# A decoder layer in split fp32r on one core: Strassen's form for four of eight row pairs, another order of the SwiGLU chunks, deeper weight staging

## The chip, the core and the metric

The kernel runs on one core of a Trainium2 chip. The metric is device time in microseconds (us) of one execution. Three runs of the kernel before took 1230.06, 1230.45 and 1231.88 us; the median is 1230.45 us.

The engines are named as the profile names them: PE (TensorE matmul; PEld is its weight load, the load of the stationary operand), DVE (VectorE), ACT (ScalarE), POOL (GpSimd), SP (the queue that issues most loads).

## The reference

One layer on x of shape (1, 256, 2048) in fp32: a norm, one projection, three mixers side by side, an output projection, and a SwiGLU block. The change lies in the SwiGLU block, the last stage:

```python
h = rms_norm(x, ffn_norm_w[l])
gate, up = jnp.split(h @ w_ffn_in[l], 2, axis=-1)     # w_ffn_in: 2048 x 11264
x = x + (jax.nn.silu(gate) * up) @ w_ffn_out[l]       # w_ffn_out: 5632 x 2048
```

## The kernel before

**Three products for one.** Every fp32 operand is cut into a rounded part `hi` (fp32r) and the rest `lo`. A product is three matmuls, hi by hi, hi by lo and lo by hi (`triple`, L1364). ACT makes `hi` of a weight tile by a cast, DVE makes `lo` by a subtraction (`split`, L1326). A weight tile `raw` has 128 rows of two times 512 columns and comes from HBM in two loads of 256 KB on SP.

**The SwiGLU block.** The 5632 hidden columns are eleven chunks of 512. For a chunk, the gate and the up columns are formed for 256 tokens, that is two halves of 128. The inner dimension of 2048 is 16 row blocks of 128, taken as eight row pairs q = 0 to 7. The first chunk is done plainly (`first_pair`, L1406: 192 matmuls). The other ten go through `pair` (L1424): tokens by columns is a 2 x 2 block product (gate and up, first and second half of the tokens), with the two blocks of a row pair as the inner two. For the row pairs in `SEVEN` it takes Strassen's form (Winograd's variant): 7 products, 21 matmuls (kind "S"). For the others it takes 8 products, 24 matmuls (kind "N", four accumulators, one of them fed with differences of the token halves, `dif_h`). The S form needs sums of weight blocks, which DVE makes (`ta`, `tb` in `stage`), and sums of token blocks (`sums_h`, `sums_l`), which `ext_job` (L1372) makes once, while the first chunk runs.

An S unit fills four of the `hi`/`lo` tiles, an N unit two, a unit of the output product (kind "P", 12 matmuls) one. There are eight tiles of each in a ring, and six `raw` tiles.

After the products of a chunk, DVE adds the seven accumulators up (`c11`, `u2`, `u3`, `c22`), ACT takes the silu of the gate, and DVE multiplies by up, at the end of `pair`. `hid_cols` (L1396) is a generator that a `tick()` after each unit advances: it turns the product by transposes on PE (two sets of four, into a `gd` bank) and splits it into `hidh` and `hidl`, the stationary operands of the output product.

**The order of the work.** The engines run their instructions in the order of the source from L1266 on (`V.on = S.on = TE.on = True`). `PARTS = (12, 8, 8, 8, 8)` groups the 44 hidden blocks: three chunks, then the four output chunks n = 0 to 3 over those blocks, and then four times two chunks and four output chunks. So a group's output product comes straight behind its last chunk:

```python
for pi, (nh, ins_, outs_) in enumerate(work):
    for c, ul in enumerate(ins_):
        ... sgs = pair(ul); spawn(hid_cols(sgs, c))
    for n in range(4):
        ... stage(u + 1); triple(...)
```

`stage(u + 1)` puts the cast and the subtraction of unit u + 1 just ahead of the matmuls of unit u in every queue, so that weights are one unit ahead.

Of the kernel before, what the change touches and what calls it, by code (L numbers as in the profile page):

```python
# [8 lines left out]
F32 = mybir.dt.float32  # L9
F32R = mybir.dt.float32r  # L10
# [5 lines left out]
P = 128  # L16
# [137 lines left out]
def trunk(tc, A, out, dbg=None):  # L154
# [48 lines left out]
    cst = pc.tile([P, CONST.shape[1]], F32, name="cst")  # L203
    vec = pc.tile([P, NV], F32, name="vec")

    def C(name):
        o, n = CCOLS[name]
        return cst[:, o:o + n]
# [165 lines left out]
    xs1 = p_l.tile([P, T], F32, name="xs1")  # L374

# [94 lines left out]
    gns = prq.tile([P, 2, 32], F32, name="gns")  # L470
# [824 lines left out]
    work = []  # L1295
    h0 = 0
    for pi, nh in enumerate(PARTS):
        ins_ = [None if h0 + c == 0 else plan_in((h0 + c) // 4) for c in range(0, nh, 4)]
        work.append((nh, ins_, [plan_out(n, h0, nh) for n in range(4)]))
        h0 += nh  # L1300

    turn = {"raw": 0, "hi": 0, "lo": 0}
    homes = {"raw": (p_raw, F32, AHEAD), "hi": (p_hi, F32R, 4), "lo": (p_lo, F32R, 4)}

    def buf(kind):
        first, dt, more = homes[kind]
        turn[kind] += 1
        if turn[kind] % 2:
            return first.tile([P, 1024], dt, tag=kind, name=nm(kind))
        return pf.tile([P, 1024], dt, tag=kind, name=nm(kind), bufs=more)  # L1310

    loaded, ready_w = {}, {}
    at = {"load": 0, "stage": 0}

    def load_upto(i):
        while at["load"] <= min(i, len(queue) - 1):
# [7 lines left out]
            at["load"] += 1  # L1324

# [8 lines left out]
    def stage(i):  # L1334
        load_upto(i + 2)
        while at["stage"] <= min(i, len(queue) - 1):
            u = at["stage"]
            kind, r = queue[u][0], loaded.pop(u)
            if kind != "S":
                parts_ = [split(t) for t in r]  # L1340
                for x in parts_:
                    x[2]()
                ready_w[u] = [half(x, j) for x in parts_ for j in range(2)]
            else:
                b11, b12 = r[0][:, 0:512], r[0][:, 512:1024]
                b22 = r[1][:, 512:1024]
                s1, s0 = split(r[1]), split(r[0], 512)
                ta = pf.tile([P, 1024], F32, tag="ta", name=nm("ta"), bufs=1)
                tb = pf.tile([P, 2, 512], F32, tag="tb", name=nm("tb"), bufs=1)
                V.tensor_tensor(ta[:, 0:512], b22, b12, op=ALU.subtract)  # L1350
                V.tensor_tensor(ta[:, 512:1024], ta[:, 0:512], b11, op=ALU.add)
                s0[2]()
                s1[2]()
                sa = split(ta)
                V.tensor_tensor(tb, r[1].rearrange("p (a c) -> p a c", c=512),
                                ta[:, 512:1024].unsqueeze(1).to_broadcast([P, 2, 512]), op=ALU.subtract)
                sb = split(tb.rearrange("p a c -> p (a c)"))
                sa[2]()
                sb[2]()
                ready_w[u] = {"b11": half(s0, 0), "b21": half(s1, 0), "b22": half(s1, 1), "t3": half(sa, 0),  # L1360
                              "t2": half(sa, 1), "t4": half(sb, 0), "t1": half(sb, 1)}
            at["stage"] += 1
# [9 lines left out]
    def ext_job():  # L1372

        for q in range(KT // 2):
            x = pf.tile([P, 1024], F32, tag="ta", name=nm("xa"), bufs=1)[:, 0:2 * T].rearrange("p (k t) -> p k t", t=T)
            s_ = pf.tile([P, 2, 512], F32, tag="tb", name=nm("xs"), bufs=1)[:, 0, :].rearrange("p (k t) -> p k t", t=P)
# [10 lines left out]
            else:  # L1387
# [3 lines left out]
                h_, l_ = dif_h[:, i], dif_l[:, i]  # L1391
            S.copy(h_, s_)
# [3 lines left out]
    def hid_cols(sgs, c):  # L1396
        for i in range(2):
            yield
            b = gdbank(1)
            turned(sgs, i, b)  # L1400
            h_ = hh_[:, 4 * c + 2 * i:4 * c + 2 * i + 2, :].rearrange("p a t -> p (a t)")
            l_ = hl_[:, 4 * c + 2 * i:4 * c + 2 * i + 2, :].rearrange("p a t -> p (a t)")
            S.copy(h_, b)
            V.tensor_tensor(l_, b, h_.bitcast(F32), op=ALU.subtract)

    def first_pair(ul):  # L1406
        ug, uu = ul
        bg = proj(ug, hx)
        sgs = []
        for t in range(2):  # L1410
            sg = pf.tile([P, 512], F32, tag=f"sg{t}", name=nm("sg"), bufs=1)
            act(sg, bg[t], AF.Silu, scale=rs2[:, t:t + 1])
            sgs.append(sg)
        banks = [mmbank(), mmbank()]
        for i in range(len(uu)):
            if i == len(uu) - 1:
                stage(0)
            products(banks, uu, i, hx)
            tick()
        for t in range(2):  # L1420
            V.tensor_tensor(sgs[t], sgs[t], banks[t], op=ALU.mult)
        return sgs

    def pair(ul):  # L1424
# [3 lines left out]
        p2, p5, p4, p3 = mmbank(), mmbank(), mmbank(), mmbank()  # L1428
# [3 lines left out]
        n_units = [q for _, q in ul if q not in SEVEN]  # L1432
        for i, (u, q) in enumerate(ul):
            stage(u + 1)
            w = ready_w.pop(u)
# [39 lines left out]
    for pi, (nh, ins_, outs_) in enumerate(work):  # L1475
        hh_ = pf.tile([P, PARTS[0], T], F32R, tag="hidh", name=nm("hidh"), bufs=1)
        hl_ = pf.tile([P, PARTS[0], T], F32R, tag="hidl", name=nm("hidl"), bufs=1)
        for c, ul in enumerate(ins_):
            if ul is None:
                ej = spawn(ext_job())  # L1480
                sgs = first_pair(plan["first"])
                finish(ej)
            else:
                sgs = pair(ul)
            spawn(hid_cols(sgs, c))
        for n in range(4):
# [67 lines left out]
```

## Time and profile before

| | us |
|---|---|
| median of three runs | 1230.45 |
| profiled execution | 1230.36 |
| its span, first to last instruction | 1228.6 |
| PE busy | 1208.6 (98%) |
| DVE busy | 900.3 (73%) |
| ACT busy | 631.4 (51%) |
| first matmul of the SwiGLU block | at 492.57 |
| last matmul | at 1223.89 |

A busy PE means that a matmul was in it; a matmul of 512 columns is recorded with 0.39 us, but the next one starts 0.23 us after it. So what a matmul costs is read from the distance of starts, and a wait from a distance that is longer. All work of this kernel is recorded at line 108 (the queue's wrapper), so rows are told apart by the names of their tiles: `hTh` and `hTl` are the normed input, `hidh` and `hidl` the hidden values, `sg` and `u` the sums at a chunk's end.

### The profile page before, as it was taken

Reading aid. Unit: us, or ns where it says so; the run is one execution under the profiler, and the core shown is the slowest. Engines: PE = TensorE matmul, PEld = TensorE weight load, DVE = VectorE, ACT = ScalarE, POOL = GpSimd, SP = SyncE. Lnnn points to the kernel's source line nnn. Section 1 sums busy time; section 2 is a strip of 40 time slices with the busy share of each in tenths; the row PEclk is TensorE's granted clock in tenths of the full one; section 3 lists DMA queues with packets and bytes.
Section 4 is the critical chain, followed back from the end, with each engine's and each line's share of the span. In section 5 each row is a group of like instructions: output and inputs, shape, how many; then the busy total and the mean of one; then the engine's idle time right before and its main releaser. Section 6 shows DMA issues by size and latency. Waiting matters only on the chain.

```text
span 1228.6 us, 16426 instructions
## 1 busy us (share of the span) xinstructions
PE 1208.6 (98%) x5972; PEld 987.6 (80%) x5972; DVE 900.3 (73%) x1249; ACT 631.4 (51%) x877; POOL 5.8 (0%) x11
## 2 busy tenths in 40 slices
PE   9999999999999999989999999999999999999998
PEld 7877888788888878778878888788877888788877
DVE  8585965699465766768975689659875888678964
ACT  7664454665446556445554355436444445445632
POOL 0100000000000000000000000000000000000000
PEclk9999999999999999999999999999999999999999
DMA  9655564256555536556556575466555656466653
GB/s 321 210 146 157 169 198 116 74 152 187 172 165 187 169 128 197 157 180 217 177 167 222 186 229 176 158 218 202 183 187 173 216 180 222 145 209 212 192 171 117
DMA packets 129058, 222.49 MB, mean 181 GB/s; under 512 B 19632, under 2 KB 23856, under 8 KB 128976
## 3 DMA queue, kind: packets, MB, share of 16 engines
q1 hardware_dynamic: 120816, 217.17, 56.6%
q10 hardware_dynamic: 8160, 4.27, 1.2%
q8 instruction: 47, 0.77, 0.3%
q14 instruction: 35, 0.29, 0.1%
HBM read 218.50 MB, written 2.88 MB: 180 GB/s over the span
## 4 chain that ended last, share of the span: by engine, by line
PE 93%; DVE 3%; ACT 2%; DMA 1%; issue 1%; SPq 0%; DVEq 0%; ACTq 0%
PE mm L108 79%; PE rw L108 8%; PE gd L108 5%; DVE lo L108 2%; ACT hi L108 1%; DMA raw<-in_w_in 0%; DVE xs L108 0%; ACT hidh L108 0%; DVE xa L108 0%; DVE sg L108 0%; DVE u L108 0%; DMA vec<-in_vecs 0%; DVE hTl L108 0%; DVE xr L108 0%; ACT s L108 0%
## 5 line engine op out<-in xcount | busy, mean ns | idle before, releaser
L108 ACT CAST hi<-raw 128x1024 fp32r<-128x1024 f32 (+2 forms) x410 | 398.4, 1004 | 266.3 <-PE mm L108 118.8
L108 DVE TENSOR_TENSOR lo<-raw,hi 128x1024 fp32r<-128x1024 f32 (+2 forms) x410 | 464.4, 1164 | 90.8 <-ACT hi L108 90.1
L108 PE MATMUL mm<-hi,hTh 128*128 128x512 f32 (+1 forms) x872 | 338.9, 395 | 2.6 <-ACT hi L108 2.5
L108 PE MATMUL mm<-lo,hTh 128*128 128x512 f32 (+1 forms) x872 | 332.9, 388 | 4.3 <-DVE lo L108 4.3
L108 PE MATMUL mm<-hi,hTl 128*128 128x512 f32 (+1 forms) x872 | 332.4, 387 | 0.0
L108 PEld LDWEIGHTS mm<-lo,hTh 128*128 128x128 f32 x872 | 162.8, 188 | 38.3 <-DVE lo L108 6.4
L108 PEld LDWEIGHTS mm<-hi,hTh 128*128 128x128 f32 x872 | 162.6, 188 | 38.4 <-ACT hi L108 4.4
L108 PEld LDWEIGHTS mm<-hi,hTl 128*128 128x128 f32 x872 | 162.6, 188 | 33.9 <-issue 0.6
L108 PE MATMUL mm<-hi,hidh 128*128 128x512 f32 x352 | 138.1, 392 | 5.4 <-ACT hidh L108 5.4
L108 PE MATMUL mm<-lo,hidh 128*128 128x512 f32 x352 | 137.7, 391 | 1.8 <-DVE lo L108 1.8
L108 PE MATMUL mm<-hi,hidl 128*128 128x512 f32 x352 | 138.0, 392 | 0.0
L108 DVE SCALAR_TENSOR_TENSOR xr<-mm,rst,xr 128x512 f32<-128x512 f32 x40 | 30.0, 750 | 73.5 <-PE mm L108 73.5
L108 PEld LDWEIGHTS mm<-hi,hidh 128*128 128x128 f32 x352 | 66.1, 188 | 20.4 <-ACT hidh L108 7.3
L108 PEld LDWEIGHTS mm<-lo,hidh 128*128 128x128 f32 x352 | 66.1, 188 | 17.5 <-DVE lo L108 4.3
L108 PEld LDWEIGHTS mm<-hi,hidl 128*128 128x128 f32 x352 | 66.1, 188 | 16.8 <-DVE hidl L108 3.4
L108 ACT CAST hi<-tb 128x1024 fp32r<-128x1024 f32 x30 | 31.6, 1054 | 55.1 <-DVE tb L108 55.1
L108 ACT CAST hi<-ta 128x1024 fp32r<-128x1024 f32 x30 | 31.6, 1054 | 42.8 <-DVE ta L108 42.7
L108 ACT ACTIVATE sg<-sg,rst 128x512 f32<-128x512 f32 x20 | 14.5, 724 | 75.1 <-DVE sg L108 75.1
L108 PE MATMUL mm<-hi,dif_l 128*128 128x512 f32 x100 | 38.9, 389 | 0.0
L108 PE MATMUL mm<-hi,dif_h 128*128 128x512 f32 x100 | 38.9, 389 | 0.0
L108 PE MATMUL mm<-lo,dif_h 128*128 128x512 f32 x100 | 38.9, 389 | 0.0
L108 DVE TENSOR_TENSOR lo<-tb,hi 128x1024 fp32r<-128x1024 f32 x30 | 36.8, 1226 | 1.4
(327 smaller groups left out, 1391.7 us busy)
## 6 DMA issues: line engine op xcount, KB each, us to landing
raw<-in_w_ffn_in SPq DMA_DIRECT2D x320, 256.0 KB, 3.9
raw<-in_w_in SPq DMA_DIRECT2D x103, 512.0 KB, 3.7
raw<-in_w_ffn_out SPq DMA_DIRECT2D x176, 256.0 KB, 4.1
raw<-in_w_out SPq DMA_DIRECT2D x32, 512.0 KB, 3.9
raw<-in_w_ffn_in SPq DMA_DIRECT2D x16, 512.0 KB, 3.7
raw<-in_w_in SPq DMA_DIRECT2D x9, 256.0 KB, 5.8
xr<-in_x SPq DMA_DIRECT2D x8, 256.0 KB, 5.4
out<-xr ACTq DMA_DIRECT2D x8, 256.0 KB, 2.0
```

The lines of the kernel that those rows point to most:

```text
L108: r = call(*a, **kw)
```

## The change

It changes five things.

1. `SEVEN` is (0, 2, 4, 6) in place of (1, 3, 5): four row pairs in Strassen's form in place of three. The order of the accumulators at a chunk's end is p2, p3, p5, p4.
2. The groups are one chunk, and then five times two. The output chunks of a group no longer follow it: two of its four come behind the first chunk of the next group, two behind the second. `hidh` and `hidl` have two buffers for that. The last group's output comes at the end.
3. Staging: `take_f` puts the cast and subtraction of as many units into the queues as fit into the eight tiles, counted with the unit that has just been used as free, where `stage(u + 1)` put one. `raw` has five tiles in place of six.
4. The two multiplications by up move from the end of `pair` (and of `first_pair`) into `hid_cols`, which runs at the first tick behind it, that is behind what `take_f` has put into the queues by then.
5. `ext_job` yields once more, between the sums of token blocks on DVE and their cast on ACT; S takes its tiles in another order; the 128 columns `ident` of the constants are a tile and a load of their own, and the rest of the constants lie in a pool that is closed before the SwiGLU block.

```diff
-AHEAD = 2
+TILES = {"raw": 1, "hi": 4, "lo": 4}
-PARTS = (12, 8, 8, 8, 8)
-SEVEN = (1, 3, 5)
+GROUPS = (1, 2, 2, 2, 2, 2)
+SEVEN = (0, 2, 4, 6)
...
-        nc.sync.dma_start(cst, A["const"])
+        nc.sync.dma_start(cst[:, 0:CONST.shape[1] - P], A["const"][:, P:])
+        nc.sync.dma_start(ident, A["const"][:, 0:P])
...
+    for gi, ng in enumerate(GROUPS):
+        for j in range(ng):
+            seq.append(("in", gi, j, None if c0 + j == 0 else plan_in(c0 + j)))
+            if gi:
+                before = GROUPS[gi - 1]
+                for n in range(4 * j // ng, 4 * (j + 1) // ng):
+                    seq.append(("out", gi - 1, n, plan_out(n, 4 * (c0 - before), 4 * before)))
+        c0 += ng
+    for n in range(4):
+        seq.append(("out", gi, n, plan_out(n, 4 * (c0 - ng), 4 * ng)))
...
+    def need(u):
+        return {"P": 1, "N": 2, "S": 4}[queue[u][0]]
+
+    def take_f(u):
+        while at["stage"] < len(queue) and (at["stage"] <= u or
+                                            at["cooked"] + need(at["stage"]) - at["used"] <= 4 + TILES["hi"]):
+            stage_one()
+        at["used"] += need(u)
+        return ready_w.pop(u)
...
-                s1, s0 = split(r[1]), split(r[0], 512)
+            s0, s1 = split(r[0], 512), split(r[1])
...
     def ext_job():
...
+            yield
             S.copy(h_, s_)
             V.tensor_tensor(l_, s_, h_.bitcast(F32), op=ALU.subtract)
             yield

-    def hid_cols(sgs, c):
+    def hid_cols(ab_, hid, c):
+        for x, y in ab_:
+            V.tensor_tensor(x, x, y, op=ALU.mult)
         for i in range(2):
             yield
             b = gdbank(1)
-            turned(sgs, i, b)
+            turned([x for x, _ in ab_], i, b)
...
-            if i == len(uu) - 1:
-                stage(0)
             products(banks, uu, i, hx)
+            if i == len(uu) - 4:
+                load()
+            if i == len(uu) - 2:
+                stage_one()
             tick()
-        for t in range(2):
-            V.tensor_tensor(sgs[t], sgs[t], banks[t], op=ALU.mult)
-        return sgs
+        return list(zip(sgs, banks))
...
-        p2, p5, p4, p3 = mmbank(), mmbank(), mmbank(), mmbank()
+        p2, p3, p5, p4 = mmbank(), mmbank(), mmbank(), mmbank()
...
-            stage(u + 1)
-            w = ready_w.pop(u)
+            w = take_f(u)
...
         V.tensor_tensor(c11, c11, p2, op=ALU.add)
+        V.tensor_tensor(u2, u2, p3, op=ALU.add)
+        act(c11, c11, AF.Silu, scale=rs2[:, 0:1])
         V.tensor_tensor(c22, u3, p5, op=ALU.add)
         V.tensor_tensor(u2, u2, p5, op=ALU.add)
         V.tensor_tensor(u3, u3, p4, op=ALU.add)
-        V.tensor_tensor(u2, u2, p3, op=ALU.add)
-        act(c11, c11, AF.Silu, scale=rs2[:, 0:1])
         act(u3, u3, AF.Silu, scale=rs2[:, 1:2])
-        V.tensor_tensor(c11, c11, u2, op=ALU.mult)
-        V.tensor_tensor(u3, u3, c22, op=ALU.mult)
-        return [c11, u3]
+        return [(c11, u2), (u3, c22)]
```

DVE's queue at the end of a chunk, before (here the second chunk that goes through `pair`): `mm` are the accumulators, `sg` and `u2` the sums, the rows with two of these on the right and no `mm` the multiplications; `lo` is the staging of later weights.

```order
L108 TENSOR_TENSOR lo_971_5647<-raw_956_5570,hi_970_5646 128x1024
L108 TENSOR_TENSOR sg_961_5602<-sg_961_5602,mm_899_5326 128x512
L108 TENSOR_TENSOR c22_972_5674<-sg_963_5604,mm_900_5327 128x512
L108 TENSOR_TENSOR u2_962_5603<-u2_962_5603,mm_900_5327 128x512
L108 TENSOR_TENSOR sg_963_5604<-sg_963_5604,mm_901_5328 128x512
L108 TENSOR_TENSOR u2_962_5603<-u2_962_5603,mm_902_5329 128x512
L108 TENSOR_TENSOR sg_961_5602<-sg_961_5602,u2_962_5603 128x512
L108 TENSOR_TENSOR sg_963_5604<-sg_963_5604,c22_972_5674 128x512
L108 TENSOR_TENSOR lo_977_5690<-raw_964_5608,hi_976_5689 128x1024
```

The same place now (the third chunk that goes through `pair`; the seven behind it read alike):

```order
L108 TENSOR_TENSOR sg_1110_6241<-u2_1109_6240,gd_1046_5942 128x512
L108 TENSOR_TENSOR lo_1112_6246<-raw_1095_6163,hi_1111_6245 128x1024
L108 TENSOR_TENSOR lo_1115_6253<-raw_1100_6174,hi_1114_6252 128x1024
L108 TENSOR_TENSOR lo_1117_6257<-raw_1101_6177,hi_1116_6256 128x1024
L108 TENSOR_TENSOR lo_1121_6267<-raw_1104_6208,hi_1120_6266 128x1024
L108 TENSOR_TENSOR sg_1108_6239<-sg_1108_6239,mm_1040_5936 128x512
L108 TENSOR_TENSOR u2_1109_6240<-u2_1109_6240,mm_1041_5937 128x512
L108 TENSOR_TENSOR c22_1122_6294<-sg_1110_6241,mm_1042_5938 128x512
L108 TENSOR_TENSOR u2_1109_6240<-u2_1109_6240,mm_1042_5938 128x512
L108 TENSOR_TENSOR sg_1110_6241<-sg_1110_6241,mm_1043_5939 128x512
L108 TENSOR_TENSOR lo_1126_6305<-raw_1107_6215,hi_1125_6304 128x1024
L108 TENSOR_TENSOR lo_1130_6315<-raw_1113_6249,hi_1129_6314 128x1024
```

Four subtractions for later weights stand ahead of the five additions, where three stood, and two between the additions and the multiplications, which are the next two rows of the queue.

DVE's queue at the end of the first chunk, before: `xa`, `xs` and `dif_l` are the token sums of `ext_job`, the rows with `sg` and `mm` the multiplications.

```order
L108 TENSOR_TENSOR dif_l_4571<-xs_790_4790,dif_h_4570 128x256
L108 TENSOR_TENSOR lo_797_4804<-raw_795_4801,hi_796_4803 128x1024
L108 TENSOR_TENSOR lo_800_4822<-raw_798_4819,hi_799_4821 128x1024
L108 TENSOR_TENSOR lo_803_4840<-raw_801_4837,hi_802_4839 128x1024
L108 TENSOR_TENSOR lo_806_4858<-raw_804_4855,hi_805_4857 128x1024
L108 TENSOR_TENSOR lo_809_4876<-raw_807_4873,hi_808_4875 128x1024
L108 TENSOR_TENSOR lo_817_4934<-raw_810_4915,hi_816_4933 128x1024
L108 TENSOR_TENSOR lo_819_4937<-raw_811_4918,hi_818_4936 128x1024
L108 TENSOR_TENSOR sg_791_4795<-sg_791_4795,mm_793_4799 128x512
L108 TENSOR_TENSOR sg_792_4797<-sg_792_4797,mm_794_4800 128x512
```

The same place now:

```order
L108 TENSOR_TENSOR tb_817_4934<-raw_807_4885,ta_816_4933 128x1024
L108 TENSOR_TENSOR lo_819_4940<-ta_816_4933,hi_818_4939 128x1024
L108 TENSOR_TENSOR lo_821_4944<-tb_817_4934,hi_820_4943 128x1024
L108 TENSOR_TENSOR xa_824_4954<-hTh_86,hTl_87 128x512
L108 TENSOR_TENSOR xs_825_4955<-xa_824_4954 128x256
L108 TENSOR_TENSOR dif_l_4574<-xs_825_4955,dif_h_4573 128x256
L108 TENSOR_TENSOR lo_836_4982<-raw_808_4888,hi_835_4981 128x1024
L108 TENSOR_TENSOR lo_838_4985<-raw_809_4891,hi_837_4984 128x1024
L108 TENSOR_TENSOR sg_783_4771<-sg_783_4771,mm_785_4775 128x512
L108 TENSOR_TENSOR sg_784_4773<-sg_784_4773,mm_786_4776 128x512
```

The multiplications now stand behind a whole S unit, the last token sums and an N unit; the bank `mm` that the first of them reads is that of the next chunk's p5.

ACT's queue during the first chunk, before: `hi` casts of weights and, between each two of them, a cast of token sums (`sums_h`, `dif_h`), which waits for DVE.

```order
L108 CAST sums_h_4568<-xs_770_4688 128x512
L108 CAST hi_772_4698<-raw_771_4696 128x1024
L108 CAST dif_h_4570<-xs_775_4715 128x256
L108 CAST hi_777_4722<-raw_776_4720 128x1024
L108 CAST sums_h_4568<-xs_780_4739 128x512
L108 CAST hi_782_4749<-raw_781_4747 128x1024
```

The same engine and stage now:

```order
L108 CAST hi_793_4804<-raw_792_4802 128x1024
L108 CAST sums_h_4571<-xs_791_4796 128x512
L108 CAST hi_796_4824<-raw_795_4822 128x1024
L108 CAST hi_801_4846<-raw_800_4844 128x1024
L108 CAST dif_h_4573<-xs_799_4841 128x256
L108 CAST hi_804_4866<-raw_803_4864 128x1024
```

Of the weight casts there are now two for one cast of token sums, and the sums that it waits for stand a unit earlier.

## Rows read from the trace of the kernel before

**Rows 1.** The page: busy time by engine, and PE's granted clock in 40 slices.

```profile
PE 1208.6 (98%) x5972; PEld 987.6 (80%) x5972; DVE 900.3 (73%) x1249; ACT 631.4 (51%) x877; POOL 5.8 (0%) x11
...
PEclk9999999999999999999999999999999999999999
```

**Rows 2.** Stretches: us; PE, PEld, DVE, ACT, POOL busy; granted clock; DMA share; GB/s.

```profile
784.11:915.67 131.56, 129.84 (x576) 106.03 (x575) 101.04 (x109) 62.96 (x70) 0.00 (x0) 1.00 0.60 192
...
492.57:1224.30 731.73, 718.46 (x3175) 585.20 (x3173) 549.34 (x605) 346.24 (x395) 0.00 (x0) 1.00 0.59 188
```

**Rows 3.** Timeline of PE within a chunk: start, duration, tiles, count.

```profile
1150.25 0.60 PE L108 MATMUL gd<-cst,sg 128*128 128x128 f32 x4
1150.61 0.48 PE L108 MATMUL rw<-hi,hTh 128*128 128x512 f32 x1
...
1152.78 0.39 PE L108 MATMUL gd<-hi,sums_h 128*128 128x512 f32 x1
...
1160.94 0.39 PE L108 MATMUL rw<-hi,hTh 128*128 128x512 f32 x1
...
1171.14 0.39 PE L108 MATMUL mm<-hi,hTh 128*128 128x512 f32 x1
```

**Rows 4.** Timeline of PE: first chunk's start, a wait, next chunk's first S unit.

```profile
492.57 0.39 PE L108 MATMUL mm<-hi,hTh 128*128 128x512 f32 x1
...
515.42 0.50 PE L108 MATMUL mm<-lo,hTh 128*128 128x512 f32 x1 [0.76 <-DVE lo L108]
...
551.16 0.39 PE L108 MATMUL rw<-hi,hTh 128*128 128x512 f32 x1
```

**Rows 5.** Timeline of ACT in the first chunk.

```profile
516.46 0.41 ACT L108 CAST dif_h<-xs 128x256 fp32r<-128x256 f32 x1 [2.35 <-DVE xs L108]
516.78 1.04 ACT L108 CAST hi<-raw 128x1024 fp32r<-128x1024 f32 x1
```

**Rows 6.** Timeline of DVE in the first chunk.

```profile
514.14 1.22 DVE L108 TENSOR_TENSOR lo<-raw,hi 128x1024 fp32r<-128x1024 f32 x1 [0.25 <-ACT hi L108]
515.28 0.68 DVE L108 TENSOR_TENSOR xa<-hTh,hTl 128x512 f32<-128x512 f32 x1
516.00 0.43 DVE L108 TENSOR_TENSOR xs<-xa 128x256 f32<-128x256 f32 x1
...
517.85 1.23 DVE L108 TENSOR_TENSOR lo<-raw,hi 128x1024 fp32r<-128x1024 f32 x1 [0.53 <-ACT hi L108]
```

**Rows 7.** Timeline of PE where a group's output product begins.

```profile
785.30 0.50 PE L108 MATMUL mm<-lo,hidh 128*128 128x512 f32 x1 [0.37 <-DVE lo L108]
...
789.21 0.50 PE L108 MATMUL mm<-hi,hidh 128*128 128x512 f32 x1 [0.68 <-ACT hidh L108]
...
793.62 0.50 PE L108 MATMUL mm<-hi,hidh 128*128 128x512 f32 x1 [0.68 <-ACT hidh L108]
```

**Rows 8.** Timeline of DVE at a chunk's end.

```profile
576.19 0.69 DVE L108 TENSOR_TENSOR u<-sg,rw 128x512 f32<-128x512 f32 x1
576.91 0.69 DVE L108 TENSOR_TENSOR sg<-u,gd 128x512 f32<-128x512 f32 x1
577.52 3.49 DVE L108 TENSOR_TENSOR lo<-raw,hi 128x1024 fp32r<-128x1024 f32 x3
...
589.76 0.69 DVE L108 TENSOR_TENSOR sg<-sg,c 128x512 f32<-128x512 f32 x1
590.36 0.68 DVE L108 TENSOR_TENSOR ta<-raw,raw 128x512 f32<-128x512 f32 x1
...
596.99 2.35 DVE L108 TENSOR_TENSOR lo<-raw,hi 128x1024 fp32r<-128x1024 f32 x2
```

**Rows 9.** Timeline of ACT at a chunk's end.

```profile
630.28 0.72 ACT L108 ACTIVATE sg<-sg,rst 128x512 f32<-128x512 f32 x1 [2.00 <-DVE sg L108]
630.91 1.98 ACT L108 CAST hi<-raw 128x1024 fp32r<-128x1024 f32 x2
```

**Rows 10.** Loads by line: count, KB each, median us from issue to landing.

```profile
raw<-in_w_ffn_in SPq DMA_DIRECT2D x320, 256.0 KB, 3.9
```

More of the change, by code (lines that the diff above doesn't have):

```diff
@@ L200, in anybank @@
         return rwbank() if tog[0] else gdbank()
-    cst = pc.tile([P, CONST.shape[1]], F32, name="cst")
+    ident = pc.tile([P, P], F32, name="ident")
+    pc.tile([P, 8], F32, name="gap0")
     vec = pc.tile([P, NV], F32, name="vec")
@@ L207, in C @@
         o, n = CCOLS[name]
-        return cst[:, o:o + n]
+        return cst[:, o - P:o - P + n]
     def vcol(name, j=0, n=1):
@@ L469, in trunk @@
     Yt = prq.tile([P, 2, 512], F32, name="Yt")
-    gns = prq.tile([P, 2, 32], F32, name="gns")
+    gns = prq.tile([P, 2, 24], F32, name="gns")
     cm_rw, pr = pool("rwp")
@@ L1293, in plan_out, with load @@
         return ul
[L1295 to L1300, printed above, removed]
+    seq = []
+    c0 = 0
+    for gi, ng in enumerate(GROUPS):
[8 more added lines that the diff above has]
+        seq.append(("out", gi, n, plan_out(n, 4 * (c0 - ng), 4 * ng)))
     turn = {"raw": 0, "hi": 0, "lo": 0}
-    homes = {"raw": (p_raw, F32, AHEAD), "hi": (p_hi, F32R, 4), "lo": (p_lo, F32R, 4)}
+    homes = {"raw": (p_raw, F32), "hi": (p_hi, F32R), "lo": (p_lo, F32R)}
     def buf(kind):
-        first, dt, more = homes[kind]
+        first, dt = homes[kind]
+        i = turn[kind] % (4 + TILES[kind])
         turn[kind] += 1
-        if turn[kind] % 2:
+        if i < 4:
             return first.tile([P, 1024], dt, tag=kind, name=nm(kind))
-        return pf.tile([P, 1024], dt, tag=kind, name=nm(kind), bufs=more)
+        return pf.tile([P, 1024], dt, tag=kind, name=nm(kind), bufs=TILES[kind])
     loaded, ready_w = {}, {}
-    at = {"load": 0, "stage": 0}
-    def load_upto(i):
-        while at["load"] <= min(i, len(queue) - 1):
+    at = {"load": 0, "stage": 0, "raw": 0, "cooked": 0, "used": 0}
+    def need(u):
+        return {"P": 1, "N": 2, "S": 4}[queue[u][0]]
+    def load():
+        while at["load"] < len(queue) and at["raw"] + len(queue[at["load"]][1]) <= 4 + TILES["raw"]:
             tiles = []
@@ L1324, in load_upto @@
             at["load"] += 1
+            at["raw"] += len(tiles)
+    def take_f(u):
[4 more added lines that the diff above has]
+        return ready_w.pop(u)
     def split(r, n=1024):
@@ L1332, in half @@
         return hl[0][:, 512 * j:512 * (j + 1)], hl[1][:, 512 * j:512 * (j + 1)]
[L1334 to L1346, printed above, removed]
-                s1, s0 = split(r[1]), split(r[0], 512)
[L1348 to L1362, printed above, removed]
@@ new lines, in stage_one @@
+    def stage_one():
+        load()
+        u = at["stage"]
+        kind, r = queue[u][0], loaded.pop(u)
+        if kind != "S":
+            parts_ = [split(t) for t in r]
+            for x in parts_:
+                x[2]()
+            ready_w[u] = [half(x, j) for x in parts_ for j in range(2)]
+        else:
+            b11, b12 = r[0][:, 0:512], r[0][:, 512:1024]
+            b22 = r[1][:, 512:1024]
+            s0, s1 = split(r[0], 512), split(r[1])
+            ta = pf.tile([P, 1024], F32, tag="ta", name=nm("ta"), bufs=1)
+            tb = pf.tile([P, 2, 512], F32, tag="tb", name=nm("tb"), bufs=1)
+            V.tensor_tensor(ta[:, 0:512], b22, b12, op=ALU.subtract)
+            V.tensor_tensor(ta[:, 512:1024], ta[:, 0:512], b11, op=ALU.add)
+            s0[2]()
+            s1[2]()
+            sa = split(ta)
+            V.tensor_tensor(tb, r[1].rearrange("p (a c) -> p a c", c=512),
+                            ta[:, 512:1024].unsqueeze(1).to_broadcast([P, 2, 512]), op=ALU.subtract)
+            sb = split(tb.rearrange("p a c -> p (a c)"))
+            sa[2]()
+            sb[2]()
+            ready_w[u] = {"b11": half(s0, 0), "b21": half(s1, 0), "b22": half(s1, 1), "t3": half(sa, 0),
+                          "t2": half(sa, 1), "t4": half(sb, 0), "t1": half(sb, 1)}
+        at["stage"] += 1
+        at["raw"] -= len(r)
+        at["cooked"] += need(u)
+        load()
@@ L1479, in trunk @@
+    hids = []
+    for what, gi, j, ul in seq:
+        if what == "in":
+            if j == 0:
+                hids.append([pf.tile([P, 8, T], F32R, tag=tag, name=nm(tag), bufs=2) for tag in ("hidh", "hidl")])
             if ul is None:
                 ej = spawn(ext_job())
-                sgs = first_pair(plan["first"])
+                ab_ = first_pair(plan["first"])
                 finish(ej)
             else:
-                sgs = pair(ul)
-            spawn(hid_cols(sgs, c))
-        for n in range(4):
+                ab_ = pair(ul)
+            spawn(hid_cols(ab_, hids[gi], j))
+        else:
+            hh_, hl_ = hids[gi]
```

37 lines of the change are left out of this document (15 added, 22 removed).

## The prediction

> **What bounds the kernel now.** I read the page first: PE is busy in 98% of the span, DVE in 73%, ACT in 51%, and PE's granted clock is full in all slices, that is the upper of its two levels, 2.4 GHz [rows 1]. Then the stretches: in the SwiGLU block PE is busy 718.46 of 731.73 us, DVE 549.34, and the loads take 0.59 of the DMA engines [rows 2]. So what counts is the number of matmuls, and the places where PE waits.
>
> Within a chunk 45 matmuls start in 10.20 us (1160.94 to 1171.14), 0.2267 us each [rows 3]. A set of four transposes takes 0.36 us (1150.25 to 1150.61), and the nine matmuls behind it 2.17 in place of 2.04: 0.49 a set [rows 3].
>
> With these two prices, the waits are what is left over:
> - First chunk: from 492.57 to the first S unit at 551.16 are 58.59 us [rows 4]. In it are 216 matmuls (48.96) and two sets of transposes (0.98). Lost: 8.65, in waits like that of 515.42. Their cause is a loop of two engines: ACT's cast of the token sums waits 2.35 for DVE's `xs`, which stands behind the last `lo`; the next weight cast stands behind that cast, the next `lo` behind the weight cast [rows 5, 6]. From `lo` to `lo` it takes 3.71 us (514.14 to 517.85); PE has used a unit up in 12 x 0.2267 = 2.72.
> - A group's end: from 784.11 to 915.67 are 131.56 us [rows 2], with 558 matmuls (2 x 183 + 192, 126.48) and four sets (1.96). Lost: 3.12, in three waits, for a `lo` and twice for `hidh` [rows 7]. There are four such groups, and the first one shows only the wait like 785.30 (0.53 and a slow restart of 0.11, since the matmul behind a wait starts 0.34 and not 0.23 after it). Together 13.1.
>
> All else in the block is PE at its pace.
>
> **The change part by part.** The sum is made against the profiled execution's 1230.36 us (1228.6 in the span, 1.8 around it); it lies at the median of the runs, 1230.45.
>
> *Strassen for one more row pair.* An S unit has 21 matmuls, an N unit 24; ten chunks save 30 x 0.2267 = 6.8 us. DVE pays: an S unit takes it 6.63 us (590.36 to 596.99 [rows 8]), an N unit two `lo` at 1.135 (577.52 has three in 3.49, the last of them 1.22 [rows 6, 8]), 2.27. That is 43.6 us more over the block, and 6 more for the eight additional accumulations. DVE had 101.04 of 131.56 us in two chunks with their output [rows 2]; it gets some 111. On the average PE hides that. Within a chunk it doesn't (four S and four N take DVE 35.6 us and the chunk's end 7, PE 40.8), but two units staged ahead (8.9 us) do.
>
> *First chunk.* The additional yield breaks the loop: a cast of token sums now finds its `xs` done. Two units then need of DVE two `lo` (2.27), `xa` 0.72, at most four token sums, none longer than the 0.43 of 256 columns (1.72), and their `lo`, 0.61 by its 512 columns: at most 5.3 us [rows 6, 8], and PE takes 5.44. The 8.65 us go; at worst they stay. I take all of them, since each row of the loop leads back to the one cast.
>
> *Output chunks behind the next group.* `hidh` is a chunk old when it is used, so the 13.1 us of the groups' ends go. What is late next is below.
>
> *Multiplications behind the staging.* This is the new price. The transposes stand in PE's queue behind two units of the next section, and PE doesn't pass them: at 515.42 what follows the late matmul waits too [rows 4]. They need the multiplications, and these wait in DVE's queue. Take the eight chunks from the third on. Let u be the start of the first sum (576.19 in [rows 8]); it follows 0.39 + 0.03 after the start of p6's last matmul, the 15th of the last S unit. From that matmul to the transposes are 6 + 24 + 24 + 1 steps, 12.47 us, so they are due at u + 12.05. On DVE: u to the second sum 0.72; to the first `lo` 0.61; four `lo` 4.54; five additions 4 x 0.61 + 0.69. That is u + 9.00. On ACT, the silu (0.63 until the next cast can start [rows 9]), the cast 1.04, two hand-overs of 0.03: u + 10.73. Two `lo`, 2.27; the first multiplication 0.69 and 0.06 to PE: u + 13.75, that is 1.70 late. The second one comes 0.60 later where 0.09 would do, 0.51, and the restart costs 0.11: 2.32 a chunk, 18.6 for eight. The bounds: with the last addition as early as p4 lets it (its last matmul plus 0.39), the wait is 0.20 + 0.51 + 0.11 = 0.82; above, each microsecond that a `lo` waits for its load comes on top. I take 2.32, which has no free number in it.
>
> Behind the first two chunks of `pair` the group has but two units in an output chunk, so a whole S unit is staged between additions and multiplications: 6.63 on DVE in place of ACT's 1.73 and the 2.27. With the earliest last addition the wait is 2.73 + 0.51 + 0.11 = 3.35, with one as late as in the other chunks 4.82. I take one of each, 8.2.
>
> Behind the first chunk the multiplication frees the bank of p5, due 15 matmuls (3.40 us) after the chunk's end. The last cast of the next S unit needs a tile of the ring that the first chunk's last unit reads, so it starts 0.19 after the end; then 1.04, `lo` 1.14, `xa` 0.72, `xs` 0.46, ACT's cast of the sums 0.32 and of the weights 1.07, two `lo` 2.27, the multiplication 0.69, with hand-overs 7.99 us. The wait is 4.6, with the restart 4.7.
>
> *The rest.* Five `raw` tiles for six: a load lands 3.9 us after its issue [rows 10], and a ring of five has at least one unit in flight while DVE stages another; nothing, by that cover (its loss is a rival). The load of the constants in two, `gns` and the pools: the first stages run at PE's pace, nothing; half a microsecond either way if not.
>
> **Sum:** 1230.36 - 6.8 - 8.65 - 13.1 + 18.6 + 8.2 + 4.7 = 1233.3 us.
>
> One rule speaks against the change beyond this. PE's granted clock was 1.00 in the whole block, where the waits were 0.7 us and the like [rows 2, 4, 7]; three of the new ones are 3 to 5 us, and no row shows what the clock does behind such a wait. The Trainium skill, "TensorE: Matmul & The Clock Gate", section "Why this matters for your kernels", says that a long idle gap between bursts of matmuls drops the clock to its lower level. By the rows the clock costs nothing, by the rule some: the second rival below.
>
> **The rivals.**
> 1. *The multiplications come almost in time (faster).* If DVE has done the four `lo` before the last matmul of p4, all waits fall to their lower bounds: 8 x 0.82 + 2 x 3.35 + 4.7 = 18.0, and the time is 1230.36 - 28.55 + 18.0 = 1219.8 us. It decides from the point where the last addition starts at the end of p4 and not 1.5 us behind. For it: DVE has a fifth of its time free [rows 2]. Against it: the `lo` stand in its queue behind a sum that PE's own p6 releases, so DVE can't run ahead there. Chance 0.13.
> 2. *The clock falls behind the long waits.* If PE runs at 1.2 GHz behind the three waits for as long as each lasted (4.6 + 4.3 + 2.7 = 11.6 us), half of that is lost: 5.8, and the time is 1239 us. Nothing of before speaks for or against it. 0.07.
> 3. *Loads come late.* With a `raw` tile less, a `lo` ahead of the additions waits for its load; one microsecond in each of eight chunks gives 1241 us. For it: landing takes 3.9 us [rows 10], and the ring holds a unit less. Against it: the DMA engines are at 0.59. 0.10.
> 4. *The first chunk keeps its waits*, because a loop of another kind forms in the order of DVE: 1242 us. Against it: at most 5.3 us of DVE in 5.44. 0.08.
>
> **How the numbers follow.** The forecast has 0.62, with its own range of 1229 to 1237: an uncertainty of a quarter in the 31.5 us of new waits and a half in the first chunk's. A measurement tells 0.2% from no change, so the limits are 1227.9 and 1232.9; of the forecast's 0.62 I put 0.01 below these limits, 0.27 between them and 0.34 above. Faster: that and rival 1, 0.14. Same: 0.27. Slower: 0.34 and rivals 2 to 4, 0.59. The range that holds 8 of 10 reaches from 1226, half way to rival 1, to 1240, between rivals 2 and 3.
>
> **What would show it.** In the profile after: 30 matmuls fewer; no wait for `hidh`; no wait of PE for `lo` in the first chunk; about 4.6 us before the first matmul of p5 behind it, ended by DVE; ten waits ahead of `gd<-ident,sg`, ended by DVE `sg`, eight of them near 1.7 us and two of 3 to 4.5; two chunks with four output chunks in about 131.7 us, as before (127.1 of matmuls and transposes and 4.6 of waits). If the transposes wait under 1 us, rival 1 holds and I mis-sized DVE's chain; if ACT waits for loads ahead of the fourth `lo`, rival 3; if a matmul behind a wait shows twice its distance, rival 2.

## The result and the profile after

The changed kernel takes 1238.67 us (median of four runs, 1237.40 to 1239.80) against 1230.26 us (four runs of the kernel before). The ratio is 1.0065, with a 95% interval from 1.0048 to 1.0083. The forecast was 1233.3 us, with a range from 1226 to 1240 and 0.59 for slower. The profiled execution took 1237.40 us, with a span of 1235.5 us and a mean granted clock of 0.995. Of six executions of one kernel below (late in eight chunks) one took 1490.33 us at a mean granted clock of 0.752, and is left out of that kernel's numbers.

The page, to be read against [rows 1]:

```profile
PE 1203.8 (97%) x5942; PEld 985.9 (80%) x5942; DVE 946.6 (77%) x1310; ACT 649.6 (53%) x897; POOL 5.8 (0%) x11
...
PEclk9999999999999999999999999999999999999999
...
PE 86%; DVE 8%; issue 3%; DMA 2%; ACT 2%; DVEq 0%; SPq 0%; ACTq 0%
```

There are 30 matmuls fewer. The last row is the chain of work that ended last: 8% of the span is now DVE's. PE's waits, summed by what ended them (engine, tile, releaser: us in all, times, longest):

```profile
PE gd L108 <- DVE sg L108: 20.4, 20, 4.3
PE mm L108 <- DVE sg L108: 4.6, 1, 4.6
...
PE mm L108 <- ACT hi L108: 1.0, 1, 1.0
```

The last row is at the program's start. There is no wait for `hidh` any more, where the kernel before waited at the groups' ends [rows 7], and none for a `lo` of the first chunk. The twenty waits ahead of transposes are two for each of ten chunks. Here are the three long ones, and one of the eight chunks behind them (PE's timeline, the first matmul behind each wait, idle time and its releaser in brackets):

```profile
545.19 0.76 PE L108 MATMUL mm<-hi,sums_h 128*128 128x512 f32 x1 [4.58 <-DVE sg L108]
...
595.23 0.30 PE L108 MATMUL gd<-ident,sg 128*128 128x128 f32 x1 [4.32 <-DVE sg L108]
...
653.14 0.30 PE L108 MATMUL gd<-ident,sg 128*128 128x128 f32 x1 [3.06 <-DVE sg L108]
...
775.40 0.30 PE L108 MATMUL gd<-ident,sg 128*128 128x128 f32 x1 [1.36 <-DVE sg L108]
775.91 0.55 PE L108 MATMUL gd<-ident,sg 128*128 128x128 f32 x3 [0.21 <-DVE sg L108]
```

The last eight chunks wait 1.35 to 1.38 us each, and 0.21 more for the second multiplication. All this stands where the prediction put it. What it did not count is what PE does behind the long waits (its timeline behind the first of them):

```profile
545.75 0.63 PE L108 MATMUL mm<-lo,sums_h 128*128 128x512 f32 x1
546.18 0.63 PE L108 MATMUL mm<-hi,sums_l 128*128 128x512 f32 x1
...
548.85 0.40 PE L108 MATMUL mm<-hi,hTh 128*128 128x512 f32 x1
549.08 0.39 PE L108 MATMUL mm<-lo,hTh 128*128 128x512 f32 x1
```

For about 3.4 us the matmuls start 0.43 us apart, and then 0.23 again. Stretches show why (us; PE, PEld, DVE, ACT, POOL busy; granted clock; DMA share; GB/s):

```profile
540.00:545.00 5.00, 0.61 (x3) 0.19 (x1) 3.97 (x7) 3.76 (x5) 0.00 (x0) 1.00 0.12 20
545.00:548.50 3.50, 3.31 (x8) 2.66 (x9) 3.46 (x6) 1.04 (x1) 0.00 (x0) 0.51 0.80 270
548.50:553.00 4.50, 4.50 (x22) 3.67 (x21) 4.44 (x5) 2.95 (x3) 0.00 (x0) 1.00 0.76 236
...
595.20:599.00 3.80, 3.56 (x11) 2.76 (x12) 2.54 (x5) 2.48 (x3) 0.00 (x0) 0.64 0.00 0
599.00:603.00 4.00, 4.00 (x20) 3.28 (x19) 3.41 (x4) 1.11 (x2) 0.00 (x0) 0.92 0.42 133
...
653.10:657.50 4.40, 4.14 (x13) 3.27 (x14) 3.14 (x5) 2.48 (x3) 0.00 (x0) 0.63 0.00 0
657.50:662.00 4.50, 4.50 (x22) 3.68 (x22) 3.30 (x5) 1.29 (x3) 0.00 (x0) 0.98 0.59 178
775.40:906.96 131.56, 128.38 (x569) 104.92 (x569) 109.01 (x119) 66.42 (x74) 0.00 (x0) 1.00 0.60 192
```

Behind each long wait, within 1.2 us of its end, the granted clock falls to its lower level, 1.2 GHz, and nowhere else in the block. The page's row of tenths hides that, since a slice of it is 31 us long. Lost are (1 - clock) times the stretch: 0.49 x 3.5 = 1.7 us, 0.36 x 3.8 + 0.08 x 4.0 = 1.7 us and 0.37 x 4.4 + 0.02 x 4.5 = 1.7 us, together 5.1 us. The last row is a whole period of two chunks: 131.56 us, as before [rows 2], where 131.7 was forecast.

### The profile page after: what moved, and what is told of

Its sections match the earlier page's. It is cut to its first block, busy times and chain, and to the rows that moved or that the text cites. A ratio compares the mean times of both kernels' runs of the same rounds, so it can differ in the third digit from the quotient of the medians.

```text
span 1235.5 us, 16564 instructions
## 1 busy us (share of the span) xinstructions
PE 1203.8 (97%) x5942; PEld 985.9 (80%) x5942; DVE 946.6 (77%) x1310; ACT 649.6 (53%) x897; POOL 5.8 (0%) x11
## 4 chain that ended last, share of the span: by engine, by line
PE 86%; DVE 8%; issue 3%; DMA 2%; ACT 2%; DVEq 0%; SPq 0%; ACTq 0%
PE mm L108 71%; PE rw L108 9%; PE gd L108 6%; DVE lo L108 4%; DVE sg L108 2%; ACT hi L108 1%; DMA raw<-in_w_ffn_in 1%; DVE u L108 1%; DMA raw<-in_w_in 0%; DVE tb L108 0%; DMA vec<-in_vecs 0%; DVE c L108 0%; ACT s L108 0%; DVE ta L108 0%; DVEq L108 0%
## 5 line engine op out<-in xcount | busy, mean ns | idle before, releaser
L108 PE MATMUL mm<-hi,hTh 128*128 128x512 f32 (+1 forms) x832 | 322.8, 394 | 1.0 <-ACT hi L108 1.0
L108 PE MATMUL mm<-lo,hTh 128*128 128x512 f32 (+1 forms) x832 | 317.1, 387 | 0.0
L108 PE MATMUL mm<-hi,hTl 128*128 128x512 f32 (+1 forms) x832 | 316.9, 387 | 0.0
L108 ACT CAST hi<-tb 128x1024 fp32r<-128x1024 f32 x40 | 42.2, 1054 | 68.8 <-DVE tb L108 67.2
L108 ACT CAST hi<-ta 128x1024 fp32r<-128x1024 f32 x40 | 42.0, 1050 | 36.5 <-DVE ta L108 34.8
L108 DVE TENSOR_TENSOR lo<-tb,hi 128x1024 fp32r<-128x1024 f32 x40 | 49.0, 1225 | 3.7 <-ACT hi L108 1.3
L108 DVE TENSOR_TENSOR tb<-raw,ta 128x1024 f32<-128x1024 f32 x40 | 48.7, 1218 | 0.0
L108 DVE TENSOR_TENSOR lo<-ta,hi 128x1024 fp32r<-128x1024 f32 x40 | 48.7, 1217 | 0.0
L108 ACT CAST hidh<-gd 128x512 fp32r<-128x512 f32 x22 | 12.9, 587 | 62.1 <-PE gd L108 62.1
L108 DVE TENSOR_TENSOR hidl<-gd,hidh 128x512 fp32r<-128x512 f32 x22 | 15.2, 692 | 35.9 <-ACT hidh L108 35.8
```

The source lines that it names most:

```text
L108: r = call(*a, **kw)
```

## The experiments

Two theories were open. The first: the sum of the prediction is right, and the clock behind the three long waits adds 5 us. The rival: the missing 5 us lie in one of its terms. So most terms were undone or done alone. Ratios are to the kernel before, run beside each.

**Early multiplications.** The two multiplications by up go back straight behind the additions; all else stays changed.

```diff
-    def hid_cols(ab_, hid, c):
+    def multiply(ab_):
         for x, y in ab_:
             V.tensor_tensor(x, x, y, op=ALU.mult)
+
+    def hid_cols(ab_, hid, c, late):
+        if late:
+            multiply(ab_)
...
-            spawn(hid_cols(ab_, hids[gi], j))
+            late = False
+            if not late:
+                multiply(ab_)
+            spawn(hid_cols(ab_, hids[gi], j, late))
```

> The changed kernel with the two multiplications of a chunk put back straight behind its additions, ahead of any staging. Theory (ten late multiplications and the first one make PE wait, and the three longest waits halve the clock for a while): the waits seen after (4.58, 4.32, 3.06, eight of 1.37, with their second halves of 0.5 and slow restarts some 29 us together) and the three stretches at half clock (some 5 us) go: 1238.7 - 34 = about 1205 us, granted clock 1.000. Rival (DVE has too much to do within a chunk, and the wait moves to the weights when the multiplications go first): PE waits for lo in place of sg, 1225 us or more.

Measured: 1210.56 us, ratio 0.9836 [0.9821, 0.9851]. The price of the late multiplications is 1238.67 - 1210.56 = 28.1 us. The theory's 1205 was 5 us short, because other waits had been behind the removed ones:

```profile
PE gd L108 <- DVE hidl L108: 3.0, 2, 2.1
PE mm L108 <- DVE sg L108: 1.7, 1, 1.7
```

These are the waits for `hidl` and for p5's bank. The second set of transposes uses the bank of the first, and `hidl`, which frees it, stands behind a whole S unit's staging; and p5's bank is still late. The clock wasn't full throughout either, as the theory had it: behind the wait of 2.13 us the profile shows one stretch at the lower level (last section).

**Which multiplications cost it.** The late ones were put back for the eight last chunks alone, and for the first three alone. Against the version with early ones (`gi` is the group; in the other kernel the condition is `gi < 2`):

```diff
-            late = False
+            late = gi > 1
```

> Multiplications early for the first chunk and the first two that go through pair, late (as in the change) for the other eight. Theory: e1 plus eight waits of 1.37 + 0.5 + 0.1, that is 1205 + 16 = 1221 us, and no stretch at half clock, since no wait is over 1.4 us. Rival (the 5 us beyond the forecast do not come from the clock but from something all through the block): 1226 us.

> Multiplications late for the first chunk and the first two that go through pair alone, early for the other eight. Theory: e1 plus waits of 4.7, 4.9 and 3.7 us plus three stretches at half clock (5 us): 1205 + 18 = 1223 us, with three stretches at half clock in the trace. Rival (the clock falls by chance or with load, not behind a long wait): 1218 us, or another count of stretches.

Measured: late in eight chunks 1226.68 us (1225.30 to 1227.67), ratio 0.9965 [0.9953, 0.9978]; late in the first three 1222.41 us, ratio 0.9934 [0.9919, 0.9949]. Above the version with early ones these are 16.1 and 11.9 us, together 28.0 of the 28.1: the two parts add up. Eight times 2.32 was forecast, 18.6 us; 16.1 is 2.0 a chunk. In the first three, waits of 4.58, 4.33 and 3.07 us stand in the place of 1.70, 2.13 and 0.85, which is 7.3 us more. The rest of the 11.9, 4.6 us, fits the clock: in this profile it loses 2.3, 2.5 and 1.5 us behind the three waits, against 1.7 behind the wait of 2.13 in the profile with early multiplications.

The totals alone would mislead here. 1226.68 is near the rival's number, and 1222.41 near the theory's, but both theories started from 1205 and the measured start was 1210.56. Taken from there, the eight chunks cost what the theory said (16.1 for 16), with a mean clock of 1.000 in the profile, and the first three less (11.9 for 18), since waits of 4.7 us had stood behind theirs. The next kernel decides between theory and rival.

**The clock alone.** The changed kernel, with the three long waits filled by matmuls whose results nobody reads. PE then isn't idle, and what comes behind still starts when DVE is done. 18 stand ahead of p5 behind the first chunk, 17 and 11 ahead of the transposes behind the first two chunks of `pair`.

```diff
+    def idle_fill(bank, n):
+        for _ in range(n):
+            TE.matmul(bank, lhsT=hTh[:, 0, 0:P], rhs=hTh[:, 0:2, :].rearrange("p k t -> p (k t)"), start=True, stop=True)
...
+            if i == 0:
+                idle_fill(b, fill)
...
+                if first and fill:
+                    idle_fill(gdbank(1), fill)
                 triple(p5, s1, w["t1"], first, last)
...
-                ab_ = pair(ul)
-            spawn(hid_cols(ab_, hids[gi], j))
+                ab_ = pair(ul, 18 if (gi, j) == (1, 0) else 0)
+            spawn(hid_cols(ab_, hids[gi], j, {(1, 0): 17, (1, 1): 11}.get((gi, j), 0)))
```

> The changed kernel, with the three long waits of PE (4.58, 4.32 and 3.06 us) filled by 18, 17 and 11 matmuls of 512 columns whose results nobody reads, shorter than the waits by their distance of starts (4.1, 3.9, 2.5 us). Theory (the waits themselves cost what the sum says, and the missing 5 us are the half clock behind them): no stretch at a granted clock under 1.00, and about 1233.7 us. Rival (the 5 us lie somewhere else, or a wait of under 1 us still drops the clock): 1238.7 us.

Measured: 1232.88 us (ten runs, 1231.90 to 1233.38), ratio 1.0017 [1.0008, 1.0027]. PE's timeline at the first of the three, and the stretches ahead of and behind it (columns as above):

```profile
540.05 0.39 PE L108 MATMUL rw<-hi,sums_l 128*128 128x512 f32 x1
540.27 4.24 PE L108 MATMUL gd<-hTh 128*128 128x512 f32 x18
545.02 0.47 PE L108 MATMUL mm<-hi,sums_h 128*128 128x512 f32 x1 [0.51 <-DVE sg L108]
545.33 0.40 PE L108 MATMUL mm<-lo,sums_h 128*128 128x512 f32 x1
```

```profile
540.20:545.00 4.80, 4.32 (x20) 3.24 (x19) 3.80 (x6) 3.78 (x5) 0.00 (x0) 1.00 0.13 32
545.00:548.50 3.50, 3.48 (x15) 2.91 (x16) 3.47 (x6) 1.05 (x1) 0.00 (x0) 1.00 0.79 258
```

p5's first matmul starts at the same place as with the idle wait (545.02 and 545.19), so DVE's lateness is unchanged, and the clock stays at 2.4 GHz, here and in the whole profile (mean 1.000). With the multiplications just as late, 5.8 us go, so the clock behind the three waits is what the forecast lacked, and the rival falls. That 1232.88 lies so close to the sum of 1233.3 is in part luck (next section).

**The additional yield, in both kernels.** First into the kernel before, together with another tile for `xs` (that of `u2`, as in the changed kernel); later out of the fastest version (below), where the yield alone goes.

```diff
-            s_ = pf.tile([P, 2, 512], F32, tag="tb", name=nm("xs"), bufs=1)[:, 0, :].rearrange("p (k t) -> p k t", t=P)
+            s_ = pf.tile([P, 512], F32, tag="u2", name=nm("xs"), bufs=1).rearrange("p (k t) -> p k t", t=P)
...
                 h_, l_ = dif_h[:, i], dif_l[:, i]
+            yield
             S.copy(h_, s_)
```

> The kernel before with the one additional yield in the job that makes the token sums. Theory (the loop of ACT and DVE through the cast of the token sums costs the first chunk 8.65 us, and the yield breaks it): 1230.3 - 8.7 = 1221.6 us. Rival (DVE has too much work in that chunk, whatever the order): 1228 to 1230 us.

> The fastest version so far (1204.35 us) without the additional yield between the sums of token blocks and their cast. Theory (the loop of ACT and DVE comes back in the first chunk, 3.7 us a unit or more against 2.72): waits of PE for lo and hi there, 8.65 to 11 us, so 1213 to 1215.5 us. Rival (weights staged deeper hide the loop): 1204.35 us.

Measured: into the kernel before, 1221.41 us, ratio 0.9924 [0.9908, 0.9941], that is 8.85 us gone where the prediction took 8.65. Of its waits, those of the first chunk are gone; those at the groups' ends stay:

```profile
PE mm L108 <- ACT hidh L108: 5.4, 8, 0.7
PE mm L108 <- DVE lo L108: 1.8, 5, 0.4
```

Out of the fastest version, 1216.40 us, ratio 0.9880 [0.9865, 0.9894]: 12.05 us dearer, 1 us above what was expected. There the loop's longest wait is 1.90 us, and the clock falls to its lower level once behind it. Deeper staging doesn't hide the loop, and the tile of `xs`, which stays there, isn't what breaks it.

**Strassen's fourth row pair.** Three in place of four in the version with early multiplications, and four in place of three in the kernel before, which is the same edit turned round.

```diff
-SEVEN = (0, 2, 4, 6)
+SEVEN = (1, 3, 5)
```

> The version with the early multiplications (1210.6 us) with three row pairs in Strassen's form, (1, 3, 5), in place of four. Theory (PE bounds the block and the deeper staging hides DVE's extra work): 30 matmuls more, 30 x 0.2267 = 6.8 us, less what of the 2.13 and 0.85 us waits goes with less staging, so 1215 to 1217.5 us. Rival (the fourth pair gains nothing, since DVE sets the pace of its staging): 1210.6 us.

> The kernel before with SEVEN = (0, 2, 4, 6) alone. Theory (with weights one unit ahead DVE can't hide a fourth S unit in each chunk, so PE waits at the chunk's ends for more than the 6.8 us that are saved): 1233 to 1240 us. Rival (DVE has a quarter of its time free, so the 30 matmuls are saved in this order as well): 1223.5 us.

Measured: with three, 1216.36 us, ratio 0.9881 [0.9867, 0.9896], so the fourth pair is worth 5.8 us in the new order (its 30 matmuls are 6.8; the clock and other waits differ between the two as well). In the kernel before it costs: 1238.82 us, ratio 1.0064 [1.0049, 1.0079]. There PE's waits are (rows as above)

```profile
PE mm L108 <- DVE lo L108: 7.0, 15, 0.8
PE mm L108 <- DVE sg L108: 6.5, 5, 1.3
...
PE mm L108 <- DVE u L108: 1.2, 5, 0.2
```

The five for `sg` are new, and so are those for `u`: at the start of a group's last chunk its accumulators aren't free. The next chunk begins with an S unit, q = 0, and its staging stands on DVE (735.45 to 742.06 in one chunk) between the first two sums and the additions that empty the banks. DVE isn't short of time there, as the theory had it: it idles just ahead of these sums.

```profile
734.13 0.69 DVE L108 TENSOR_TENSOR u<-sg,rw 128x512 f32<-128x512 f32 x1 [4.20 <-PE rw L108]
```

The number came out as expected, but what these waits show is the order of DVE's queue. So four pairs at these places lose by themselves; four that begin with an N unit were not tried.

**A better version.** Early multiplications; the token sums two steps earlier; and two banks for the two sets of transposes, where an output chunk follows and p7's bank lies free. Against the version with early multiplications:

```diff
-                ej = spawn(ext_job())
+                ej = spawn(ext_job(), 2)
...
-            b = gdbank(1)
+            b = gdbank(i if other else 1)
...
-            spawn(hid_cols(ab_, hids[gi], j, late))
+            spawn(hid_cols(ab_, hids[gi], j, late, gi > 0))
```

> The version with the early multiplications (1210.6 us), with the token sums made one unit earlier (two steps of ext_job ahead of the first chunk), and the two sets of transposes of a chunk in two banks where an output chunk follows. Theory: the waits of 1.70, 2.13 and 0.85 us go, and with them the one stretch at half clock that was seen: 1205 to 1206.5 us. Rival (the waits only move to the next matmul that DVE feeds): 1209 to 1211 us.

Measured: 1204.35 us (four runs, 1204.30 to 1204.55), ratio 0.9784 [0.9769, 0.9799]: faster than both kernels. PE's waits that are left beside the program's start:

```profile
PE mm L108 <- DVE xr L108: 0.4, 1, 0.4
...
PE mm L108 <- DVE sg L108: 0.3, 1, 0.3
PE mm L108 <- DVE lo L108: 0.2, 1, 0.2
```

The prediction's three savings alone, 1230.36 - 6.8 - 8.65 - 13.1, are 1201.8 us. The version lies 2.5 us above that: of the 28.55 us some 26 are there together.

**The order of the sections.** The better version, with each group's output chunks straight behind it.

```diff
-GROUPS = (1, 2, 2, 2, 2, 2)
+GROUPS = (3, 2, 2, 2, 2)
...
-            if gi:
-                before = GROUPS[gi - 1]
-                for n in range(4 * j // ng, 4 * (j + 1) // ng):
-                    seq.append(("out", gi - 1, n, plan_out(n, 4 * (c0 - before), 4 * before)))
         c0 += ng
-    for n in range(4):
-        seq.append(("out", gi, n, plan_out(n, 4 * (c0 - ng), 4 * ng)))
+        for n in range(4):
+            seq.append(("out", gi, n, plan_out(n, 4 * (c0 - ng), 4 * ng)))
...
-                hids.append([pf.tile([P, 8, T], F32R, tag=tag, name=nm(tag), bufs=2) for tag in ("hidh", "hidl")])
+                hids.append([pf.tile([P, 12, T], F32R, tag=tag, name=nm(tag), bufs=1) for tag in ("hidh", "hidl")])
...
-            spawn(hid_cols(ab_, hids[gi], j, late, gi > 0))
+            spawn(hid_cols(ab_, hids[gi], j, late, j == GROUPS[gi] - 1))
```

> The fastest version so far (1204.35 us) with the old order of the sections: groups of 3, 2, 2, 2 and 2 chunks, each followed at once by its four output chunks; all else as it is. Theory (the order is worth more than the 13.1 us of the sum: two chunks in a row ask DVE for 2 x 42.6 us while PE needs 2 x 40.8, and the second one's staging and end come late; an output chunk between them gives DVE the time): PE waits 2.5 to 4 us at a chunk's end and ahead of the output product in every group, and 1240 to 1255 us. Rival (the order is worth the 13.1 us of the sum): 1217.5 us.

Measured: 1266.24 us, ratio 1.0284 [1.0262, 1.0306], 61.9 us above the better version and 11 beyond the expectation. PE's waits, and DVE's timeline ahead of one of those for `sg`:

```profile
PE mm L108 <- DVE sg L108: 35.1, 10, 3.7
PE mm L108 <- ACT hidh L108: 5.4, 8, 0.7
```

```profile
734.20 0.69 DVE L108 TENSOR_TENSOR u<-sg,rw 128x512 f32<-128x512 f32 x1 [5.49 <-PE rw L108]
734.92 0.69 DVE L108 TENSOR_TENSOR sg<-u,gd 128x512 f32<-128x512 f32 x1
735.53 0.68 DVE L108 TENSOR_TENSOR ta<-raw,raw 128x512 f32<-128x512 f32 x1
...
742.15 2.35 DVE L108 TENSOR_TENSOR lo<-raw,hi 128x1024 fp32r<-128x1024 f32 x2
744.42 0.68 DVE L108 TENSOR_TENSOR sg<-sg,mm 128x512 f32<-128x512 f32 x1
```

The waits come to 40.5 us. The mean clock of 0.984 over a span of 1265.2 us is another 20. The waits were in the theory, the clock was not. The theory's cause was half wrong: DVE isn't overloaded there, since it idles 5.49 us just before. What counts is its queue: the deeper staging has put an S and an N unit, 8.9 us, between the first sums and the additions, and the next chunk waits for the banks that these empty. An output chunk that follows instead puts four `lo` there, 4.5 us, and takes two banks of the four. With three row pairs, which begin with an N unit, the old order was not tried beside the deeper staging.

## Why the prediction came out as it did

*First chunk, -8.65.* Right: 8.85 us, measured by itself. The loop was the cause, as read from ACT's and DVE's rows [rows 5, 6].

*Fourth row pair, -6.8.* Right for this order (5.8 us measured; with three pairs the clock fell behind two waits of 1.9 us). The prediction's remark that two units staged ahead are what hides DVE's work within a chunk is not shown: the kernel before with four pairs and one unit ahead is 8.0 us slower, but its new waits come from the order of DVE's queue, behind an idle DVE.

*Groups' ends, -13.1.* No wait for `hidh` is left; the 13.1 us were not measured by themselves. Beside this staging and four row pairs the new order is worth more: without it the better version loses 61.9 us, which the prediction did not see.

*Late multiplications, +18.6, +8.2 and +4.7.* Right in place, cause and nearly in size (the eight chunks cost 16.1). The chain through DVE and ACT can be followed in the trace of after, for the chunk with the transposes at 775.40:

```profile
761.62 0.69 DVE L108 TENSOR_TENSOR u<-sg,rw 128x512 f32<-128x512 f32 x1 [0.66 <-PE rw L108]
762.35 0.69 DVE L108 TENSOR_TENSOR sg<-u,gd 128x512 f32<-128x512 f32 x1
762.95 4.62 DVE L108 TENSOR_TENSOR lo<-raw,hi 128x1024 fp32r<-128x1024 f32 x4
...
772.29 2.36 DVE L108 TENSOR_TENSOR lo<-raw,hi 128x1024 fp32r<-128x1024 f32 x2 [1.73 <-ACT hi L108]
774.57 0.69 DVE L108 TENSOR_TENSOR sg<-sg,u 128x512 f32<-128x512 f32 x1
```

With u at 761.62, the forecast put the two `lo` at u + 10.73 = 772.35 and the transposes at u + 13.75 = 775.37; they start at 772.29 and 775.40. From the distance of starts, the wait ahead of p5 is 545.19 - 540.23 - 0.23 = 4.7 us, as forecast.

*The clock, taken at nothing.* This is the step that failed: "By the rows the clock costs nothing, by the rule some", and the forecast went by the rows. But these held only waits of 0.7 us and the like, and said nothing of waits of 3 to 5. Each of the three was followed by a stretch at 1.2 GHz; the cost is 5.1 us by the trace and 5.8 by the filled waits. The Trainium skill, "TensorE: Matmul & The Clock Gate", section "Why this matters for your kernels", says that a long idle gap between bursts of matmuls drops the clock; the trace agrees, with 0.51 granted behind 4.58 us of waiting. The second rival had the mechanism, at a chance of 0.07, and it was no rival but a term of the sum: 1233.3 + 5.8 = 1239.1, measured 1238.67. That its 5.8 us agree is luck: it let the slow stretch last as long as the wait, and the rows show 1.7 us lost behind each, for 4.58, 4.32 and 3.06 us of waiting alike.

In the rest of the sum two misses of 2.5 us cancel: the eight late chunks cost 16.1 us in place of 18.6, and the better version, with hardly a wait left, shows 2.5 us less than the 28.55 of the three savings. Where these 2.5 us went stays open.

*The other rivals.* The multiplications did not come almost in time: 1.36 us of idle time ahead of the transposes, where under 1 was the sign. Loads cost nothing, though the sign named for that rival was there: in seven of the eight chunks ACT waits 0.9 to 2.3 us for a load before it casts for the fourth `lo` (1.64 us until 764.49 in the chunk above). But DVE's four `lo` run without a gap in all eight, and the two `lo` behind wait for ACT's cast, which follows the silu. Loads land 3.2 us after their issue (3.9 before, [rows 10]). The first chunk did not keep its waits.

## What to carry to other kernels

Moving work off the end of a section is only a gain if what it releases isn't queued behind staging that the same section adds: find for each moved instruction what its engine has to do first, and who waits. A new wait on TensorE can cost more than its length: look at the granted clock behind it (1.7 us lost behind each of the three long ones here). Parts of a change can depend on each other: here the fourth row pair lost 8.0 us by itself and gained 5.8 beside the other parts, and the deeper staging with four pairs lost 61.9 us where no output chunks stand between the others.

## What was not expected of the hardware

Of PE's waits, those of 1.35 to 1.39 us were never followed by a stretch at 1.2 GHz, and those of 3.06 us or more always, in the three profiles that had them (the changed kernel, late in the first three chunks, the old order of the sections). Between these, and below them, the length alone doesn't decide. Waits of 1.64 and 1.70 us were not followed by one, two of 1.90 and one of 1.91 were (with three row pairs, and without the yield). In the old order of the sections, one wait of 3.04 us was followed by a full clock; the stretch behind it stands under it:

```profile
1072.05 0.47 PE L108 MATMUL mm<-hi,hidh 128*128 128x512 f32 x1 [3.04 <-DVE sg L108]
```

```profile
1072.00:1077.00 5.00, 4.95 (x22) 4.15 (x23) 4.56 (x7) 3.34 (x5) 0.00 (x0) 1.00 0.67 232
```

And a wait of 2.13 us was followed by the lower level in one kernel and not in another, where the work around it is the same:

```profile
593.10:597.10 4.00, 3.94 (x13) 3.26 (x14) 4.00 (x6) 1.62 (x3) 0.00 (x0) 0.57 0.11 21
```

```profile
592.20:596.20 4.00, 3.93 (x20) 3.32 (x21) 4.00 (x6) 2.08 (x4) 0.00 (x0) 1.00 0.11 22
```

The first is the version with early multiplications, the second the one with late multiplications in eight chunks, both from the end of that wait on. Even a wait of 1.29 us can be followed by it. In the kernel before with four row pairs such waits (1.29 and 1.30 us, with 0.22 or 0.23 more three matmuls on) stand at five places; at 875.61 the clock falls behind one, at 742.79 and the other three it doesn't:

```profile
700.00:750.00 50.00, 48.30 (x211) 38.89 (x210) 45.33 (x51) 26.02 (x30) 0.00 (x0) 1.00 0.55 176
```

```profile
875.60:880.00 4.40, 4.15 (x11) 3.02 (x12) 4.29 (x7) 3.33 (x5) 0.00 (x0) 0.67 0.04 14
```

What decides stays open. The stretch can also be longer for the same wait: with late multiplications in the first three chunks, 7.30 us from 544.70 on had a clock of 0.69, a loss of 2.3 us where the changed kernel lost 1.7.
